# Delta rule's q, k and v turned by 32x32 blocks on DVE and over DRAM instead of by TensorE, with a new slab order

## The chip, the cores and the metric

The kernel runs on one core of a Trainium2 chip. The core has TensorE (PE in the profile, with its weight loads as PEld), VectorE (DVE), ScalarE (ACT), GpSimd (POOL) and SyncE (SP), which here only issues DMAs. Each works through its own instructions in program order. The metric is the device time of one execution in microseconds (us), given as the median of several runs.

## The reference

One layer of a hybrid encoder for 512 tokens and a model width of 1024, in float32. A single projection of the normalised input gives all branches; the two branches are merged, projected, and a gated embedding is added.

```python
h = rms_norm(x, norm_pre)
(aq, ak, av, az, dq, dk, dv, db, da, dz, gate_att, gate_dn) = split_cols(h @ w_in)
# branch A: GQA, 8 heads, 2 kv heads, rotary, softmax, * silu(az), @ w_br_att
# branch B, 8 heads of 128:
qkv = silu(short_conv(concat([dq, dk, dv]), conv_w))      # depthwise, 5 taps
qd = l2_norm(heads(cq)) * 128 ** -0.5
kd = l2_norm(heads(ck))
vd = heads(cv)
o_dn = chunk_gated_delta_rule(qd, kd, vd, g[0], beta[0]) + flip(chunk_gated_delta_rule(flipped ...))
y_dn = (rms_norm(o_dn, dn_norm) * silu(dz)) @ w_br_dn
mix = (sigmoid(gate_att) * y_att + sigmoid(gate_dn) * y_dn) @ w_out
x = x + rms_norm(mix, norm_post)
x = x + rms_norm(sigmoid(x @ w_ple_gate) * (p @ w_ple_proj), ple_norm)
```

The delta rule works in chunks. Within a chunk it inverts a unit triangular matrix built from k kᵀ, beta and the decay; between chunks it carries a state. It therefore needs k and v in two forms or in the one that the convolution doesn't give: the convolution and the products k kᵀ and k qᵀ want the channel on the partitions, the scans want the token there, and the l2 norm is a sum over channels.

## The kernel before, in words

**Precision.** A large product is made of three matmuls: each float32 operand is split into a high part (`hi`, rounded to fp32r) and a remainder (`lo`), and lo·hi, hi·lo and hi·hi are summed. `gemm_t` (L529 to L531) does so for a *slab*: 128 output columns for all 512 tokens, eight steps of three 128x512 matmuls, the result with channels on partitions and tokens along the row. Weights come by DMA into `wraw`, ACT rounds them into `whi`, and DVE or POOL subtracts to give `wlo` (L102 or L97).

**Order.** No loop of the hardware sets the order. While the program is written, a planner (`Flow`) keeps a clock and a calendar of each engine. Each part of the kernel is a generator that asks for a time (`at`), for an event of another part (`ev`) or for a buffer (`get`); the part with the smallest priority number that can go on goes on. An operation is entered at the first free place of its engine, with a duration written in the code, and the instructions come out in that order. `ORDER` lists the slabs of the main stream, which has the last priority and fills PE wherever nothing else is ready; `PR` holds priorities; `COOL` and `HOT` say how much later DVE may be than POOL before a weight split goes to POOL, outside and inside of the substitution.

**Branch B.** Heads 0 to 3 are group 0, heads 4 to 7 group 1. `conv_job` multiplies the slab of one head's q, k or v; `conv_tail` then works on the 128 channels x 512 tokens in PSUM:

1. `conv_silu2`: five taps (ACT one, DVE four), tanh on ACT, one product on DVE. The result stays with channels on partitions, in `kT` or `qT`, or in a tile `f2` for v.
2. `transposed` (L758 to L764): four PE transposes of 128x128 into one PSUM bank of the pool `mm`.
3. For q and k, ACT squares the transposed bank and DVE sums over channels (`ssk`, `ssq`); for k, ACT also copies the bank to `kn`. For v, DVE multiplies the bank by the norm `nk` of k into `nv`.

`k_stats` and `q_stats` make the norms of a group of four heads out of the sums, on POOL. `phase_a` then multiplies k kᵀ and k qᵀ (L942, L947), scales by the decay, inverts 32x32 blocks by a *substitution* of 30 steps of two DVE instructions (L975, L977), with a trip through DRAM ahead (`dB`) and behind (`dW`), and joins the blocks by small matmuls (L1019, L1032, L1052, L1067). `phase_b` is the scan of four chunk pairs in each direction (L1101 to L1162); it reads `kn` and `nv`, and puts its right side r and the product w into tiles of the pool `c2` (four buffers). Group 1 follows when group 0 is done. Slabs of the main stream stand between all of these on PE.

The step on which the rest depends most closely: the first matmul of the joined blocks, L1019, waits for DVE's transposes of the blocks that come back from DRAM.

Of the kernel before, what the change touches and what calls it, by code (L numbers as in the profile page):

```python
# [17 lines left out]
NT = 4  # L18
# [17 lines left out]
class Flow:  # L36
# [87 lines left out]
    def run(self):  # L124
        while self.parts:
# [38 lines left out]
ydn4 ydn3 ydn6 ydn0 ydn1 yatt5 yatt2 yatt6 yatt1 yatt7 yatt0 yatt4 yatt3 out0 out1 pg0  # L164
pg1
"""
OUT0 = 'ydn4 ydn3 ydn0 ydn0'
# [12 lines left out]

@with_exitstack
def layer(ctx, tc, x, xT, pw0, wp1, wt, wba, wn, rows, qkn, hd16, npost, pnorm, dnorm, cs, out):
# [39 lines left out]
    def const(shape, name, dt=F32):  # L222
        return sb.tile(shape, dt, tag=name, bufs=1, name=name)
# [50 lines left out]
                           pattern=[[pat, 128]], channel_multiplier=cm)  # L274
        return m

    two = const([64, 32], "two")
    pool.tensor_add(two, ident[0:64, 0:32], ident[0:64, 32:64])
    m_le = mask("m_le", -1, 1, 0)
    m_ge = mask("m_ge", 1, -1, 0)  # L280
    m_gt = mask("m_gt", 1, -1, -1)
# [451 lines left out]
        return max(t, te)  # L733


    ssk = const([128, 2, 4, 4], "ssk")
    ssq = const([128, 2, 4, 4], "ssq")
# [20 lines left out]
    def transposed(src):  # L758
        yield "get", "mm"
        o = bank("mm", [128, 4, 128])  # L760
        for c in range(NT):
            pe.transpose(o[:, c, :], src[:, c * 128:(c + 1) * 128], ident)
        yield "pe", 0.436
        return o  # L764

    def sumsq(pt, dst, dep=0.0):
# [4 lines left out]
        free("f2", t)  # L771
        return ta, t

    def conv_tail(kind, hd, po, nke):
        g, h = hd // 4, hd % 4
        yield "get", "f2"
        y = tile("f2", [128, 512])
        if kind == "dv":
            yield "get", "f2"
            dst = tile("f2", [128, 512])  # L780
            row = 16 + hd
        else:
# [4 lines left out]
        yield "at", t + 0.3  # L787
        pt = yield from transposed(dst)
        if kind == "dv":
            free("f2")  # L790
# [5 lines left out]
        ta, t = yield from sumsq(pt, (ssk if kind == "dk" else ssq)[:, g, :, h])  # L796
        if kind == "dk":
            ta = A(0.5, ta, act.copy, kn[g][:, :, h, :], pt)
        free("mm", ta)
        return t  # L800

    def k_stats(g, evs, dec):
        for e in evs:
            yield "ev", e
        yield "ev", dec
        t = G(0.2, 0.0, pool.tensor_scalar, out=nk[:, g], in0=ssk[:, g], scalar1=4.0 * EPS, scalar2=None, op0=ALU.add)
# [11 lines left out]
    def q_stats(g, evs):  # L818
        for e in evs:
            yield "ev", e  # L820
        return rsqrt(16, 0.0, rq[:, g], 1.0, 4.0 * EPS, float(128 ** -0.5), ssq[:, g])

    conv_ev, stat_ev = {}, {}
    conv_ready = {(k, g): Event() for k in ("dk", "dq", "dv") for g in range(2)}
# [41 lines left out]
    def prep(g, d):  # L866
# [11 lines left out]
        for c in range(NT):  # L878
# [23 lines left out]
                t = Q(2, t, E1[c], E)  # L902
            tE[g, d, c] = t
        if away:
            free("u16", t)
# [19 lines left out]
    def phase_a(g):  # L925
# [8 lines left out]
        for h in range(4):  # L934
            yield "ev", conv_ev["dq", 4 * g + h]
        k_, q_ = kT[g], qT[g]
        for c in range(NT):
            cc = slice(c * 128, (c + 1) * 128)
            yield "get", "aux"
            kk = bank("aux", [128, 4, 128])  # L940
            for h in range(4):
                pe.matmul(kk[:, h, :], k_[:, h, cc], k_[:, h, cc], start=True, stop=True)  # L942
            yield "pe", 0.9
            yield "get", "aux"
            qk = bank("aux", [128, 4, 128])
            for h in range(4):
                pe.matmul(qk[:, h, :], k_[:, h, cc], q_[:, h, cc], start=True, stop=True)  # L947
            yield "pe", 0.9
            for d in range(2):
                E = LT[d][:, 4 * c:4 * c + 4, :]  # L950
                t = V(0.62, tE[g, d, c], dve.tensor_mul, AT[g][d][:, 4 * c:4 * c + 4, :], qk, E)
                t = V(0.62, t, dve.tensor_mul, E, kk, E)
            free("aux", t)
            free("aux", t)

        dB, dW = dram(f"dB{g}", [128, 32, 32]), dram(f"dW{g}", [128, 32, 32])
        yield "get", "c2"
# [29 lines left out]
        free("blk", t)  # L987
        free("blk", t)
        free("blk", t)
        VT = []  # L990
        for i in range(2):
            yield "get", "blk"
            VT.append(tile("blk", [128, 16, 64]))
            G(0.95, 0.0, pool.memset, VT[i], 0.0)
        cx, tx = [], []
        for i in range(2):
            yield "get", "c2"
# [4 lines left out]
        for q in range(4):  # L1002
            r, lc = r32(q), r32(q % 2)
            t0 = A(0.53, tx[0], act.copy, LT[0][r, :, r], cx[0][r])
            t1 = V(0.6, tx[0], dve.transpose, VT[0][r, :, lc], cx[0][r])
        free("c2", max(t0, t1))
        for q in range(4):
            r, lc = r32(q), r32(q % 2)
            t0 = A(0.53, tx[1], act.copy, VT[1][r, :, lc], cx[1][r])
            t1 = V(0.6, tx[1], dve.transpose, LT[1][r, :, r], cx[1][r])  # L1010
        free("c2", max(t0, t1))
        yield "at", max(t0, t1) + 0.3

        combos = [(0, 0, 1), (0, 2, 3), (1, 1, 0), (1, 3, 2)]
        yield "get", "aux"
# [69 lines left out]
    def phase_b(g, d, ae, st8):  # L1085
        yield "ev", ae
        yield "ev", conv_ready["dv", g]
        for h in range(4):
            yield "ev", conv_ev["dv", 4 * g + h]
        yield "ev", stat_ev["q", g]  # L1090
        o = oo[g]
        tS = 0.0
# [320 lines left out]

    def q_done():
        for b in range(2):
            for t in range(NT):
# [8 lines left out]
    sm = const([128, 4, 4, 8], "sm")  # L1425
    ya = [None, None]

    def att_head(h):
# [485 lines left out]
```

## Time and profile before

| | |
|---|---|
| median of 3 runs | 762.31 us (762.13 to 762.71) |
| the profiled execution | 762.67 us, span 760.9 us |
| granted TensorE clock | 0.997 of full speed |
| DMA | 102.59 MB in 54472 packets, mean 135 GB/s |

The profile is of one execution. "Busy" is the time in which an engine worked on an instruction; matmuls overlap, so the distance between their starts tells more of PE than their durations. Rows of groups read: line, engine, operation, output<-input, shapes, count, then busy us and mean ns of one, then the idle time of that engine just before them and what ended it. The chain of waits is followed back from the last instruction. Line 122 and line 102 are those of helpers that record most operations, so such rows are told apart by their tiles.

### The profile page before, as it was taken

The page shows a single profiled execution, that of the slowest core. Times are in us where ns is not written, and L with a number is a line of the kernel's source. Part 1 is how long each engine was busy: PE and PEld are TensorE (multiplying, and loading weights), DVE is VectorE, ACT ScalarE, POOL GpSimd, SP SyncE. Part 2 cuts the span into 40 slices and gives each one's busy share as a digit, 9 for nine tenths or more (in the row PEclk, how much of TensorE's full clock was granted, in tenths as well). Part 3 has the DMA queues.
Part 4 walks back from the last instruction along what each step waited for, and adds up shares of the span by engine and source line. Part 5 has one row for each costly group of instructions (what it writes and reads, how often), then busy time and mean ns, then how long its engine had stood idle before and what let it go on. Part 6 is the DMA issues. An engine that isn't in the chain of part 4 may idle for free.

```text
span 760.9 us, 11834 instructions
## 1 busy us (share of the span) xinstructions
PE 746.0 (98%) x4505; PEld 624.7 (82%) x4505; DVE 465.1 (61%) x906; ACT 345.7 (45%) x644; POOL 307.8 (40%) x277
## 2 busy tenths in 40 slices
PE   8999999999999999999999999999999999999995
PEld 7788888878789888888798888888888888888885
DVE  4587788796955667894864535447666743313434
ACT  6668535543644264424442245335665623332422
POOL 4845762003322264202711246657454434661501
PEclk9999999999999999999999999999999999999998
DMA  9861338618111237554311134425335255552323
GB/s 346 300 196 60 113 92 280 205 61 235 39 61 42 70 111 189 178 167 118 113 56 42 56 103 134 158 91 194 111 97 166 72 193 205 187 169 104 97 72 108
DMA packets 54472, 102.59 MB, mean 135 GB/s; under 512 B 21072, under 2 KB 22032, under 8 KB 54416
## 3 DMA queue, kind: packets, MB, share of 16 engines
q1 hardware_dynamic: 54128, 101.58, 41.3%
q8 instruction: 35, 0.57, 0.3%
q10 hardware_dynamic: 288, 0.26, 0.1%
q14 instruction: 21, 0.17, 0.1%
HBM read 82.92 MB, written 18.91 MB: 134 GB/s over the span
## 4 chain that ended last, share of the span: by engine, by line
PE 88%; DMA 3%; DVE 3%; ACT 2%; issue 1%; POOL 1%; SPq 0%; POOLq 0%; DVEq 0%; ACTq 0%
PE mm L529 16%; PE mm L531 16%; PE mm L530 16%; PE mm L550 4%; PE mm L549 4%; PE mm L548 4%; PE mm L567 2%; PE mm L568 2%; PE mm L566 2%; PE aux L1121 2%; PE mm L1476 2%; PE aux L1153 2%; PE aux L1101 1%; PE aux L1112 1%; PE aux L1139 1%
## 5 line engine op out<-in xcount | busy, mean ns | idle before, releaser
L102 POOL TENSOR_TENSOR wlo<-wraw,whi 128x1024 fp32r<-128x1024 f32 x52 | 124.7, 2397 | 255.9 <-ACT whi L122 225.3
L529 PE MATMUL mm<-u,wlo 128*128 128x512 f32 x504 | 204.7, 406 | 2.2 <-DVE f L122 1.2
L531 PE MATMUL mm<-u,whi 128*128 128x512 f32 x504 | 197.2, 391 | 0.0
L530 PE MATMUL mm<-u,whi 128*128 128x512 f32 x504 | 196.5, 390 | 0.0
L529 PEld LDWEIGHTS mm<-u,wlo 128*128 128x128 f32 x504 | 94.8, 188 | 21.2 <-issue 2.0
L531 PEld LDWEIGHTS mm<-u,whi 128*128 128x128 f32 x504 | 94.6, 188 | 20.8
L530 PEld LDWEIGHTS mm<-u,whi 128*128 128x128 f32 x504 | 95.0, 188 | 17.0
L122 ACT CAST whi<-wraw 128x1024 fp32r<-128x1024 f32 x64 | 67.2, 1050 | 86.7 <-PE mm L531 55.8
L122 DVE SCALAR_TENSOR_TENSOR f<-mm,cw,f 128x510 f32<-128x510 f32 (+1 forms) x96 | 71.7, 747 | 20.7 <-ACT f L122 18.1
L102 POOL TENSOR_TENSOR u<-wraw,u 128x1024 fp32r<-128x1024 f32 x23 | 55.1, 2399 | 21.5 <-ACT u L122 21.4
L122 DVE TENSOR_TENSOR u<-aux,u 128x512 f32<-128x512 f32 (+2 forms) x60 | 39.3, 670 | 23.7 <-ACT u L122 15.4
L548 PE MATMUL mm<-u,u 128*128 128x512 f32 (+1 forms) x136 | 52.0, 382 | 0.0
L550 PE MATMUL mm<-u,u 128*128 128x512 f32 (+1 forms) x136 | 51.4, 378 | 0.0
L549 PE MATMUL mm<-u,u 128*128 128x512 f32 (+1 forms) x136 | 51.3, 377 | 0.0
L122 ACT COPY c<-aux 128x512 f32<-128x512 f32 x18 | 10.6, 590 | 55.0 <-DVE f L122 35.0
L122 ACT CAST u<-aux 128x512 fp32r<-128x512 f32 (+1 forms) x28 | 15.6, 556 | 39.9 <-PE aux L1649 13.0
L122 ACT ACTIVATE f<-mm 128x512 f32<-128x512 f32 (+1 forms) x38 | 21.1, 566 | 23.5 <-PE mm L550 8.7
L566 PE MATMUL mm<-whi,u 128*128 128x512 f32 x80 | 31.6, 395 | 0.0
L567 PE MATMUL mm<-wlo,u 128*128 128x512 f32 x80 | 31.3, 391 | 0.0
L568 PE MATMUL mm<-whi,u 128*128 128x512 f32 x80 | 31.2, 390 | 0.0
L122 ACT ACTIVATE mm<-f 128x512 f32<-128x512 f32 x24 | 14.5, 602 | 34.3 <-DVE f L122 33.0
L550 PEld LDWEIGHTS mm<-u,u 128*128 128x128 f32 x136 | 25.6, 188 | 4.8
(255 smaller groups left out, 1452.6 us busy)
## 6 DMA issues: line engine op xcount, KB each, us to landing
wraw<-in_wt_dram SPq DMA_DIRECT2D x60, 512.0 KB, 3.5
wraw<-in_wn_dram SPq DMA_DIRECT2D x28, 512.0 KB, 3.9
u<-in_wt_dram SPq DMA_DIRECT2D x12, 512.0 KB, 5.7
u<-CI SPq DMA_DIRECT2D x16, 256.0 KB, 6.3
u<-in_x_dram SPq DMA_DIRECT2D x4, 512.0 KB, 6.9
u<-in_xT_dram SPq DMA_DIRECT2D x4, 512.0 KB, 8.2
eD<-u SPq DMA_DIRECT2D x8, 256.0 KB, 8.0
gate_dz<-go SPq DMA_DIRECT2D x8, 256.0 KB, 2.1
```

The costliest lines, as they stand in the source:

```text
L102: ins = fn(*a, **k)
L122: fn(*a, **k)
L529: pe.matmul(o, lo[:, k, :], mh(k), start=(k == 0), stop=False)
L530: pe.matmul(o, hi[:, k, :], ml(k), start=False, stop=False)
L531: pe.matmul(o, hi[:, k, :], mh(k), start=False, stop=(k == 7))
L548: pe.matmul(o, b, hi, start=(i == 0), stop=False)
L549: pe.matmul(o, a, lo, start=False, stop=False)
L550: pe.matmul(o, a, hi, start=False, stop=(i == 7))
L566: pe.matmul(o[t], b, hi, start=(k == 0), stop=False)
L567: pe.matmul(o[t], a, lo, start=False, stop=False)
L568: pe.matmul(o[t], a, hi, start=False, stop=(k == 7))
L1121: pe.matmul(pw[:, h, :], Vm[g][d][:, 4 * c + h, :], r[:, h, :], start=True, stop=True)
```

## The change

- The 24 conv tails have no PE transposes any more. DVE transposes the 128x512 result in 32x32 blocks (`small_blocks`): in each 32-row strip of channels, every 32 tokens become rows.
- For k and v this tile `T` is written to DRAM with 2 KB per partition, and read back by four DMAs, one for each 32-row strip of the target, in pieces of 512 bytes, into a *landing* tile (`turned`). The landing tile is taken from the pool `c2`. From there ACT or POOL copies k to `kn` (`land_k`), and ACT (four instructions with a scale per partition) or POOL multiplies v by `nk` into `nv`, both in the layout that the scans read.
- The sums of squares are taken of the block-transposed tile: ACT squares, DVE sums 32 channels at a time into partial sums (`partk` for k, the tile `sm` for q). Once for each group and kind, four fp32 matmuls with the 128x32 selector `four` add up the four strips and give [token, head] sums in a PSUM bank (`sums`). DVE reads the bank into `nk` or `rq`.
- `phase_b` also waits for the copies of k (`kn_ev`).
- Some times that the planner hands on are now the latest of several (`ready`, `tm`, `tv`), where it was the last one entered.
- The slab order, `OUT0`, the priorities and `HOT` have new numbers.

```diff
 ORDER = """
-dq3 dk2 dq2 dk0 dk3 dq0 dk1 dq1 dz2 dk7 dq6 dz3 dv2 dv1 dv3 dz0
-dq4 gB7 dz7 dv0 dz5 az5 gA6 gA0 dz1 dq5 dk5 dk4 gA1 dk6 gA7 gA3
-dq7 gB0 az7 gB6 gB1 dv4 az6 dv6 gB2 gA2 az2 gB4 kv dv7 dv5 gB5
-az0 gA4 vec dz4 az3 gB3 q0 dz6 gA5 q1 az4 az1 free_h ydn2 ydn5 ydn7
...
+dk0 vec dk1 dq0 dq1 dq3 dq2 dk2 az4 dk3 dv1 dv3 dq5 dv0 dq7 dz7
+dk5 dv2 az3 dz5 dz3 az6 gB2 gB4 dz0 az0 gA3 dk4 dk7 dz4 dq6 dq4
+gA4 dk6 gA6 gB5 dz1 dz2 dv7 dv4 dv5 gA0 az1 gA5 gB0 gA2 dv6 az2
+gA1 kv gA7 gB7 az7 gB6 gB3 q0 gB1 dz6 q1 az5 free_h ydn0 ydn6 ydn7
...
-PR = dict(dec=6, dm1=5, y=2, conv=9, gate=1, kv=2, q=4, head=9, ple=6, prep=6, tab=2)
+PR = dict(dec=8, dm1=8, y=7, conv=9, gate=0, kv=9, q=4, head=6, ple=1, prep=2, tab=1)
+WIDE = 2.0
+LAND = "c2"
-COOL, HOT = 2.5, 0
+COOL, HOT = 2.5, -1.5
...
+    def small_blocks(src, dep):
+        T = tile("f2", [128, 4, 4, 32])
+        return T, V(0.64, dep, dve.transpose, T.rearrange("p a j q -> p j a q"), src)
+
+    def turned(T, dep, name, dst):
+        B = dram(name, [4, 32, 4, 128])
+        tw = Q(2, dep, B.rearrange("P i a n -> (P i) a n"), T.rearrange("p a j q -> p a (j q)"))
+        t = tw
+        for a in range(4):
+            t = Q(WIDE, tw, dst[32 * a:32 * a + 32].rearrange("p P j q -> p P (j q)"), B[:, :, a, :].rearrange("P i n -> i P n"))
+        return tw, t
...
-        pt = yield from transposed(dst)
+        yield "get", "f2"
+        T, t = small_blocks(dst, t)
         if kind == "dv":
-            t = V(0.62, 0.0, dve.tensor_mul, nv[g][:, :, h, :], pt,
-                  nk[:, g, :, h].unsqueeze(2).to_broadcast([128, 4, 128]))
-            free("mm", t)
+            yield "get", LAND
+            L = tile(LAND, [128, 4, 4, 32])
+            tw, t = turned(T, t, f"B{kind}{hd}", L)
...
+            t = either(t, ("POOL", 1.1, pool.tensor_mul, o_, i_, nk[:, g, :, h]...),
+                       ("ACT", 1.25, scaled))
...
+        ta = A(0.5, t, act.activation, sq, T, AF.Square)
+        t = V(0.62, ta, dve.reduce_sum, parts_[kind][:, g, :, h, :], sq, axis=AX.X)
...
+    def sums(kind, g):
+        yield "at", F.now + 0.3
+        yield "get", "mm"
+        o = bank("mm", [128, 16])
+        for a in range(4):
+            pe.matmul(o[32 * a:32 * a + 32, :], four, parts_[kind][:, g, a].rearrange("p h j -> p (h j)"), start=True, stop=True)
+        yield "pe", 0.44
+        return o.rearrange("p (h j) -> p j h", h=4)
```

Three places of the new order bear on the prediction.

**PE, a conv tail's transposes and what replaces them.** Before, PE has the four transposes of v's tile `f_189` in the midst of a slab (`mm_1582` is the slab's bank; "waits" names the engine waited for):

```order
L531 MATMUL mm_1582<-u_14_130,whi_1527 128x512
L762 MATMUL mm_1603<-ident,f_189_1530 128x128 [waits DVE_49,PE_49]
L762 MATMUL mm_1603<-ident,f_189_1530 128x128 x3
L529 MATMUL mm_1582<-u_15_131,wlo_1528 128x512
L530 MATMUL mm_1582<-u_17_133,whi_1527 128x512
```

Now a slab runs on, and once per group and kind there are the selector's matmuls:

```order
L536 MATMUL mm_998<-u_14_131,whi_943 128x512
L862 MATMUL mm_1018<-partk,four 32x16 [waits DVE_49,PE_49]
L862 MATMUL mm_1018<-partk,four 32x16 x3
L534 MATMUL mm_998<-u_14_131,wlo_944 128x512
L535 MATMUL mm_998<-u_16_133,whi_943 128x512
```

All 24 blocks of L762 are gone, and four groups like the second have come.

**DVE, between the steps of group 0's substitution.** Before, early steps (L975, L977) with a conv tail (`f_159`), v's product with `nk`, a decay add (L893), a gate (`go`) and a weight split among them:

```order
L977 TENSOR_TENSOR blk_1153<-blk_1153,blk_1154 128x29x2 [waits DVE_49]
L122 SCALAR_TENSOR_TENSOR f_160_1243<-mm_1195,f_159_1242 128x512 [waits Activation_49]
L122 TENSOR_TENSOR u_136_1088<-mm_1256,nk 128x4x128 [waits PE_49]
L893 TENSOR_TENSOR u_155_1224<-u_155_1224,cj 128x512 [waits Pool_49]
L122 SCALAR_TENSOR_TENSOR go_1306<-go_1306,mm_1244 128x512 [waits DMAHW0_49]
L97 TENSOR_TENSOR wlo_1305<-u_29_210,whi_1304 128x1024 [waits DMAHW4_49,PE_49,Activation_49]
L975 TENSOR_TENSOR blk_1154<-blk_1152,blk_1153 128x28x3 [waits DVE_49]
```

Now, with the steps at L1049 and L1051:

```order
L97 TENSOR_TENSOR wlo_1460<-wraw_1314,whi_1459 128x1024 [waits DMAHW5_49,Activation_49]
L122 SCALAR_TENSOR_TENSOR go_1461<-go_1461,mm_1407 128x512 [waits Activation_49]
L1049 TENSOR_TENSOR blk_1329<-blk_1327,blk_1328 128x28x3 [waits DVE_49]
L1051 TENSOR_TENSOR blk_1328<-blk_1328,blk_1329 128x28x3 [waits DVE_49]
L1049 TENSOR_TENSOR blk_1329<-blk_1327,blk_1328 128x27x4 [waits DVE_49]
L1051 TENSOR_TENSOR blk_1328<-blk_1328,blk_1329 128x27x4 [waits DVE_49]
```

In the 30 steps there are now 8 splits, 5 gates and 6 decay adds and no conv tail; before there were 10 splits, 12 taps and 4 last products of conv tails, 4 gates, 4 decay adds, 3 products with `nk` and a sum. On PE, between the last k qᵀ product of group 0 and the first product of the joined blocks, there were 375 matmuls of 512 columns and 24 transposes, and there are now 318 matmuls of 512 columns.

**DVE and POOL, the scan's first r and the landing buffers.** On DVE the scan of group 0 begins (L1181 writes r into `c_274`), with waits for four DMA queues and POOL:

```order
L122 TENSOR_TENSOR f_265_2288<-aux_2281,dj 128x512 [waits Activation_49]
L122 TENSOR_TENSOR f_268_2297<-aux_2290,dj 128x512 [waits DMAHW1_49,Activation_49]
L1181 SCALAR_TENSOR_TENSOR c_274_2327<-aux_2322,nec,u_99_845 128x128 [waits DMAHW5_49,DMAHW6_49,DMAHW0_49,DMAHW7_49,PE_49,Pool_49]
L1181 SCALAR_TENSOR_TENSOR c_274_2327<-aux_2322,nec,u_99_845 128x128 x3
L122 SCALAR_TENSOR_TENSOR f_278_2339<-mm_2158,cw,f_278_2339 128x510 [waits Activation_49]
```

On POOL, the copies that set the landing buffers `c_238` and `c_250` (k of two heads of group 1) free stand behind weight splits:

```order
L102 TENSOR_TENSOR wlo_1963<-wraw_1852,whi_1962 128x1024 [waits DMAHW5_49,Activation_49,Pool_49]
L102 TENSOR_TENSOR wlo_2156<-u_29_211,whi_2155 128x1024 [waits DMAHW6_49,Activation_49]
L102 COPY u_158_1248<-c_238_1922 128x4x128 [waits DMAHW6_49,DMAHW7_49,DMAHW5_49,DMAHW0_49]
L102 COPY u_158_1248<-c_250_2122 128x4x128 [waits DMAHW4_49,DMAHW5_49,DMAHW3_49,DMAHW2_49]
L102 TENSOR_TENSOR wlo_2338<-wraw_2038,whi_2337 128x1024 [waits PE_49,DMAHW1_49,Activation_49,Pool_49]
```

Before, the scans shared `c2` with no landing.

More of the change, by code (lines that the diff above doesn't have):

```diff
@@ L275, in mask @@
         return m
-    two = const([64, 32], "two")
-    pool.tensor_add(two, ident[0:64, 0:32], ident[0:64, 32:64])
+    four = const([128, 32], "four")
+    pool.tensor_add(four, ident[:, 0:32], ident[:, 32:64])
+    for i in (2, 3):
+        pool.tensor_add(four, four, ident[:, 32 * i:32 * i + 32])
+    two = four[0:64, :]
     m_le = mask("m_le", -1, 1, 0)
@@ L795, in conv_tail @@
             return t
-        ta, t = yield from sumsq(pt, (ssk if kind == "dk" else ssq)[:, g, :, h])
         if kind == "dk":
-            ta = A(0.5, ta, act.copy, kn[g][:, :, h, :], pt)
-        free("mm", ta)
-        return t
+            yield "get", LAND
+            L = tile(LAND, [128, 4, 4, 32])
+            tw, t2 = turned(T, t, f"B{kind}{hd}", L)
+            spawn(land_k(hd, L, t2), PR["conv"])
+            yield "at", t - 0.2
+            yield "get", "f2"
+            sq = tile("f2", [128, 4, 4, 32])
+        else:
+            sq = T
@@ new lines, in conv_tail, with land_k @@
+        ta = A(0.5, t, act.activation, sq, T, AF.Square)
+        if kind == "dk":
+            free("f2", max(ta, tw))
+        t = V(0.62, ta, dve.reduce_sum, parts_[kind][:, g, :, h, :], sq, axis=AX.X)
+        free("f2", t)
+        return t
+    kn_ev = [Event() for _ in range(8)]
+    def land_k(hd, L, t):
+        yield "at", t - 0.5
+        o = kn[hd // 4][:, :, hd % 4, :].rearrange("p j (P q) -> p j P q", P=4)
+        t = either(t, ("ACT", 0.57, act.copy, o, L.rearrange("p P j q -> p j P q")), ("POOL", 0.7, pool.tensor_copy, o, L.rearrange("p P j q -> p j P q")))
+        free(LAND, t)
+        kn_ev[hd].set(t)
@@ L804, in k_stats @@
             yield "ev", e
+        o = yield from sums("dk", g)
+        t = V(0.2, 0.0, dve.tensor_scalar, out=nk[:, g], in0=o, scalar1=4.0 * EPS, scalar2=None, op0=ALU.add)
+        free("mm", t)
         yield "ev", dec
-        t = G(0.2, 0.0, pool.tensor_scalar, out=nk[:, g], in0=ssk[:, g], scalar1=4.0 * EPS, scalar2=None, op0=ALU.add)
         t = V(0.25, t, dve.reciprocal, kinv[:, g], nk[:, g])
@@ L820, in q_stats @@
             yield "ev", e
-        return rsqrt(16, 0.0, rq[:, g], 1.0, 4.0 * EPS, float(128 ** -0.5), ssq[:, g])
+        o = yield from sums("dq", g)
+        t = V(0.2, 0.0, dve.tensor_copy, rq[:, g], o)
+        free("mm", t)
+        return rsqrt(16, t, rq[:, g], 1.0, 4.0 * EPS, float(128 ** -0.5))
     conv_ev, stat_ev = {}, {}
@@ L904, in prep @@
         if away:
+            t = max(tE[g, d, c] for c in range(NT))
             free("u16", t)
@@ L936, in phase_a @@
         k_, q_ = kT[g], qT[g]
+        ready = 0.0
         for c in range(NT):
@@ L948, in phase_a @@
             yield "pe", 0.9
+            tm = 0.0
             for d in range(2):
```

46 lines of the change are left out of this document (30 added, 16 removed).

## The prediction

> **What bounds the kernel now.** I read the page first (busy time, slices, chain), then PE's waits, then the timelines of the places that the change touches.
>
> The page's head, busy time by engine, PE's and DVE's slices, and the chain's shares by engine:
>
> ```profile
> span 760.9 us, 11834 instructions
> PE 746.0 (98%) x4505; PEld 624.7 (82%) x4505; DVE 465.1 (61%) x906; ACT 345.7 (45%) x644; POOL 307.8 (40%) x277
> ...
> PE   8999999999999999999999999999999999999995
> ...
> DVE  4587788796955667894864535447666743313434
> ...
> PE 88%; DMA 3%; DVE 3%; ACT 2%; issue 1%; POOL 1%; SPq 0%; POOLq 0%; DVEq 0%; ACTq 0%
> ```
>
> PE is busy in every slice but the first and the last, and the chain that ended last runs through it for 88%. A busy PE may still stand behind a pipelined matmul, so I ask how fast it issues, and what it waited for (us in total, times, longest):
>
> ```profile
> PE mm L762 <- DVE f L122: 1.5, 1, 1.5
> PE mm L1777 <- POOL ident masks.py:199: 1.4, 1, 1.4
> PE mm L529 <- DVE f L122: 1.2, 1, 1.2
> PE mm L529 <- DVE wlo L97: 0.5, 2, 0.3
> ```
>
> These are the largest of nine rows. So PE has almost no idle time: the kernel is bound by the number of PE instructions, and what leaves PE shortens it one for one, unless PE waits somewhere new. What shortens DVE, ACT or POOL is worth nothing by itself.
>
> **What the change removes from PE.** Each of the 24 conv tails (q, k, v of 8 heads) now has four 128x128 transposes by matmul at L762. Around one block (start, duration):
>
> ```profile
> 55.82 0.39 PE L530 MATMUL mm<-u,whi 128*128 128x512 f32 x1
> ...
> 56.96 0.60 PE L762 MATMUL mm<-ident,u 128*128 128x128 f32 x4
> 57.31 0.48 PE L529 MATMUL mm<-u,wlo 128*128 128x512 f32 x1
> 57.62 0.39 PE L530 MATMUL mm<-u,whi 128*128 128x512 f32 x1
> ```
>
> The first two rows are five 512-column matmuls apart, 1.14 us, so one takes 0.228. From L762's start to the second matmul behind it are 0.66 us; less one matmul, the block costs 0.43. The chain of waits books it the same way (start, us, what), and L762's own rows give the count, 64 + 32:
>
> ```profile
> 57.12 0.44 PE mm L762 x4
> ...
> L762 PE MATMUL mm<-ident,u x64: 270/272/327, 38.1 to 266.5; 128*128 128x128 f32 x64
> L762 PE MATMUL mm<-ident,f x32: 270/272/328, 117.2 to 389.2; 128*128 128x128 f32 x32
> ```
>
> 24 x 0.44 = **-10.6 us**. With them goes L762's one wait for DVE, **-1.5 us** (bounds 0, if DVE's lateness shows at the next dependent instruction, and -1.5).
>
> **What it adds to PE.** Four groups of four fp32 matmuls with the 32-column selector `four` (L862, a new line), which fold the partial sums of squares. No row has this shape. Chain rows of small fp32 matmuls, in which one written matmul is two instructions:
>
> ```profile
> 40.79 0.81 PE aux L701 x8
> ...
> 200.76 0.81 PE aux L1032 x54
> ```
>
> At L701's pace (128 weight columns, 32 moving) a group of 8 instructions is 0.81 us; at L1032's (32x32) it is 8 x 0.015 = 0.12. Four groups: 0.5 to 3.2. K is 128 as in L701, so I take 0.81: **+3.2 us**.
> The Trainium skill, page "TensorE: Matmul & The Clock Gate", section "LDWEIGHTS (loading the stationary operand)", says that loading weights takes time by their columns, P / 1.2 ns, whatever K is: 107 ns for 128 columns, which the trace's 0.10 per instruction of L701 bears out, but 27 ns for 32. By that rule the term would be an estimated 0.9 us, and the sum below 2.3 us lower.
>
> **What it adds elsewhere.** Nearest rows on DVE: the block transpose (of 32 partitions), the multiply by nk that goes, the sum that stays, and a conv tap:
>
> ```profile
> L122 DVE STREAM_TRANSPOSE blk<-c 32x512 f32<-32x512 f32 x8 | 5.6, 702 | 8.4 <-DMA c<-dW 8.3
> L122 DVE TENSOR_TENSOR u<-mm,nk 128x512 f32<-128x512 f32 x8 | 5.5, 682 | 0.3 <-PE mm L762 0.3
> L122 DVE TENSOR_REDUCE ssk<-f 128x4 f32<-128x512 f32 x8 | 5.4, 680 | 0.2 <-ACT f L122 0.2
> L122 DVE SCALAR_TENSOR_TENSOR f<-mm,cw,f 128x510 f32<-128x510 f32 x48 | 35.7, 745 | 19.1 <-ACT f L122 18.1
> ```
>
> DVE: 24 x 0.70 - 8 x 0.68 = +11.4 us; the lanes work side by side in every other row, so 128 partitions should cost what 32 do (bounds: 0.70, and four times that if not). v's scaling moves to ACT, four pieces per head as at L918; k's copies, one per head as now, go to ACT or POOL, where the nearest row is a 128x512 TENSOR_SCALAR:
>
> ```profile
> L918 ACT ACTIVATE u<-u,Nj 128x128 f32<-128x128 f32 x44 | 13.2, 388 | 0.0
> ...
> L102 POOL TENSOR_SCALAR u<-u,sm 128x512 f32<-128x512 f32 x16 | 11.1, 697 | 22.5 <-DVE sm L122 16.3 <-PE aux L1468 6.0
> ```
>
> 32 x 0.39 = +12.4 us on ACT, four copies of 0.7 on POOL. All of this, POOL's two more adds for `four` and four 128x16 reads of the folded sums on DVE lie under PE's 98% and cost nothing while DVE (61%) and ACT (45%) keep ahead. If DVE's cover were gone, up to its 11.4 us would reach PE. The tables of numbers act through the order alone and are costed there, below.
>
> The landing: k and v go to DRAM (256 KB) and back in four reads of 64 KB, 80 more issues on SP. Nearest rows (KB each, us to landing):
>
> ```profile
> gate_dz<-go SPq DMA_DIRECT2D x8, 256.0 KB, 2.1
> gi<-gate_dz SPq DMA_DIRECT2D x8, 256.0 KB, 4.2
> dW<-blk SPq DMA_DIRECT2D x2, 512.0 KB, 3.4
> c<-dW SPq DMA_DIRECT2D x4, 256.0 KB, 5.1
> ```
>
> 2.1 + 4.2 to 5.1 = 6.3 to 7.2 us. Each first read waits on SP for its write, and behind it stand the next weight fetch or gate store. PE's nine waits name no DMA and weights come slabs ahead, so 2 us on SP cost 0 (bounds 0 and 2.1 per head, if that lead is gone). Only the scans read the landed k and v, tens of us after the last v of their group: 0; the price if a scan waits is in the last rival.
>
> **Where a stall can come back: the substitution of group 0.** The slab order moves conv tails away from it. In the present kernel PE's last q-k products of group 0 (L947) and the first product of the inverted blocks (L1019) stand here, DVE's last transposes before L1019 next, then DVE's busy time in three legs (start of the products to the first step, the 30 steps, the way back through DRAM), then the steps' two instructions in the middle leg, and one row of that leg:
>
> ```profile
> 105.41 1.05 PE L947 MATMUL aux<-u,u 128*128 128x128 f32 x8
> ...
> 196.54 1.29 PE L1019 MATMUL aux<-blk,u 32*32 32x32 f32 x128
> ...
> 193.70 2.89 DVE L122 STREAM_TRANSPOSE u<-c 32x512 f32<-32x512 f32 x4
> ...
> 106.40:122.00 15.60, 13.39 (x19) 1.00 0.74 212
> 122.00:180.00 58.00, 49.53 (x100) 1.00 0.53 178
> 180.00:196.60 16.60, 9.99 (x15) 1.00 0.47 115
> ...
> 122.00:180.00 58.00, 9.86 (x30) 1.00 0.53 178
> ...
> 122.00:180.00 58.00, 9.88 (x30) 1.00 0.53 178
> ...
> L893 DVE TENSOR_TENSOR u<-u,cj 128x512 f32<-128x512 f32 x4 | 2.8, 690 | 3.8 <-POOL u L102 3.6
> ```
>
> L1019 starts as DVE ends (196.6): no slack now. The order holds 375 matmuls of 512 columns and six transpose blocks between the two: 375 x 0.228 + 6 x 0.44 = 88 us of PE work as cover for a chain of 90 us. In the changed order it is 318 matmuls, 72.5 us. The chain shrinks too: the steps' leg has 49.5 - 9.9 - 9.9 = 29.8 us of other DVE work now; the new order leaves 8 weight splits, 5 gates and 6 decay adds there:
>
> ```profile
> L97 DVE TENSOR_TENSOR wlo<-wraw,whi 128x1024 fp32r<-128x1024 f32 x12 | 14.9, 1239 | 3.4 <-ACT whi L122 3.4
> L122 DVE SCALAR_TENSOR_TENSOR go<-go,mm 128x512 f32<-128x512 f32 x24 | 16.3, 681 | 5.7 <-ACT go L122 5.5 <-DMA go<-gate_gB 0.2
> ```
>
> 8 x 1.24 + 5 x 0.68 + 6 x 0.69 = 17.5 us. The first leg gains two block transposes and two sums less one multiply, 1.4 + 1.4 - 0.7 = +2.1, of which part fits its 2.2 us of idle: take +1.5. So the chain needs 15.6 + 1.5 + 19.7 + 17.5 + 16.6 = 70.9 us plus idle time between the steps. That is 8.5 us now (58.0 - 49.5); L893's wait for POOL is 3.8 of it and stays, the rest may go. With 3.8, 74.7 against 72.5: PE waits **+2.2 us** (bounds 0 and, with all 8.5, 6.9). For group 1 the order gives the opposite: 327 matmuls and 16 transposes instead of 288 and 24, 8 us more cover, and 6 us more DVE work. No term.
>
> **Sum.** -10.6 - 1.5 + 3.2 + 2.2 = -6.7 us. The profiled execution took 762.67, the median is 762.31, 0.36 lower: 762.31 - 6.7 = **755.6 us**. Start and tail keep their instructions: 0.
>
> **Rivals.**
> (1) *More goes than I count* (17%): the selector matmuls at L1032's pace (0.5) and no wait at the substitution: -10.6 - 1.5 + 0.5 = -11.6, **750.7**. For it: the weights are 32 columns wide. Against it: every fp32 row with K = 128 stands at 0.10 per instruction.
> (2) *The wait takes the place of the transposes* (12%): the substitution keeps all its idle time (6.9) and DVE's lateness of 1.5 shows there instead: -10.6 + 3.2 + 6.9 = -0.5, **761.8**, no change that can be told. For it: no slack at L1019 now, and 15.6 us less PE work in front. Against it: 12.3 us less DVE work between the steps.
> (3) *The landing buffers hold up the scan* (11%), slower. The landing tiles are taken from the four `c2` buffers in which the scans put r and w. In the new order DVE's first r of group 0 takes the buffer of the landing of one k of group 1, which POOL copies out behind a weight split:
>
> ```profile
> L102 POOL TENSOR_TENSOR wlo<-wraw,whi 128x1024 fp32r<-128x1024 f32 x52 | 124.7, 2397 | 255.9 <-ACT whi L122 225.3
> ```
>
> If that r comes before the landing has begun, PE waits for write, read, split and copy, 2.1 + 5.1 + 2.4 + 0.7 = 10.3 us: -6.7 + 10.3 = +3.6, **765.9**. It decides above 6.7 us. Against it: by the order's matmuls some 20 us of PE work lie between that k's transpose and that r, twice the price.
> The Trainium skill speaks against the change here: "VectorE: DVE Perf Modes", section "The three transpose paths", keeps 128x128 transposes for TensorE and calls a strided plain DMA 19 times slower than the crossbar's. No run here shows that factor: c<-dW, rearranged in 128-byte pieces, lands in 5.1 us against 4.2 for gi<-gate_dz in long ones.
>
> **How the numbers follow.** The forecast case has 60%, 752.5 to 759.5, for the price of the selector and the idle time. With (1) at 750.7 and most of (2), the range is **749.5 to 761.9**; it leaves out (3) and the edges. This kernel's measurement tells some 0.2%, 1.5 us, from no change: faster means below 760.8. The forecast and (1) are faster, and of (2) a part: 80%. Same, most of (2): 9%. Slower, (3): 11%.
>
> **What would show it.** L762's counterpart has no conv rows; L862 stands 32 times, in four groups of 0.8 us. PE's instructions fall by 64. PE's waits show one row of about 2 us at the first product behind the substitution (L1094 or its neighbour), none for a landing. The block transpose at 128 partitions takes 0.70 us, and the landing 6 to 7. The forecast is wrong if PE's idle time grows by more than 6 us, at the substitution or in the scans.

## The result, and the profile after

| | before | after |
|---|---|---|
| median | 762.22 us (761.99 to 762.71) | 755.03 us (754.48 to 755.96) |
| ratio to before, 95% interval | | 0.9906 (0.9889 to 0.9923) |
| profiled span | 760.9 us | 754.2 us |

The change makes the kernel 7.2 us faster; 755.6 was predicted. The head of the page of the changed kernel, its slices of PE and of the granted TensorE clock (PEclk, in tenths) and the shares of its chain, to be set against the lines of before:

```profile
span 754.2 us, 11916 instructions
PE 738.5 (98%) x4441; PEld 618.3 (82%) x4441; DVE 475.3 (63%) x924; ACT 353.2 (47%) x668; POOL 315.6 (42%) x284
...
PE   9999999999799999999999999999999999999996
...
PEclk9999999999899999999999999999999999999999
...
PE 85%; DVE 4%; DMA 4%; ACT 3%; issue 1%; POOL 1%; SPq 0%; POOLq 0%; DVEq 0%; ACTq 0%
```

PE has the 64 instructions less that the change promises (96 transposes go, 32 selectors come) and is still busy for 98%. One slice has fallen to 7, the eleventh (188 to 207 us), where the substitution of group 0 comes back. The granted clock has a dip in the same slice; before, only the last slice had one. PE's waits in the changed kernel, all rows (us in total, times, longest):

```profile
PE mm L534 <- POOL wlo L102: 2.8, 2, 2.3
PE aux L1094 <- ACT blk L122: 1.8, 2, 1.0
PE mm L1853 <- POOL ident masks.py:199: 1.4, 1, 1.4
PE aux L1107 <- issue: 1.0, 1, 1.0
PE mm L534 <- DVE wlo L97: 0.5, 2, 0.3
PE mm L656 <- POOL u L102: 0.4, 1, 0.4
PE aux L1215 <- ACT c L122: 0.3, 1, 0.3
```

They add up to 8.2 us; the nine rows of before had 6.7. L762's wait is gone, and so is the 1.2 us at L529 behind DVE. In their place two new ones stand side by side at the substitution: L1094, the first product of the inverted blocks, behind ACT's copies, and a slab's first matmul (L534) behind POOL's part of its weight split. The new work by its own rows, one group of selector matmuls within a slab and then the block transposes of q and k on DVE:

```profile
82.39 0.39 PE L536 MATMUL mm<-u,u 128*128 128x512 f32 x1
82.71 0.26 PE L862 MATMUL mm<-sm,four 128*32 128x16 f32 x8
82.89 0.50 PE L534 MATMUL mm<-u,wlo 128*128 128x512 f32 x1
83.23 0.39 PE L535 MATMUL mm<-u,whi 128*128 128x512 f32 x1
```

```profile
L122 DVE STREAM_TRANSPOSE f<-u 128x512 f32<-128x512 f32 x16 | 11.2, 702 | 0.0
```

From the matmul in front of the group to the second one behind it are 0.84 us, where two undisturbed steps take 0.46, so the group costs 0.38 us; the other three, read in the same way, cost as much. The block transpose takes 0.70 us on 128 partitions, as predicted from 32. The landing takes about what was estimated: the writes 2.3 to 2.8 us, each read 2.2 to 2.5 us (medians from issue to landing), and the fourth read is issued 1.3 us behind the first, which makes 6.1 to 6.3 us against 6.3 to 7.2.

### The profile page after: what moved, and what is told of

It reads as the page before. It is cut to its first block, busy times and chain, and to the rows that moved or that the text cites. A ratio compares the mean times of both kernels' runs of the same rounds, so it can differ in the third digit from the quotient of the medians.

```text
span 754.2 us, 11916 instructions
## 1 busy us (share of the span) xinstructions
PE 738.5 (98%) x4441; PEld 618.3 (82%) x4441; DVE 475.3 (63%) x924; ACT 353.2 (47%) x668; POOL 315.6 (42%) x284
## 4 chain that ended last, share of the span: by engine, by line
PE 85%; DVE 4%; DMA 4%; ACT 3%; issue 1%; POOL 1%; SPq 0%; POOLq 0%; DVEq 0%; ACTq 0%
PE mm L534 14%; PE mm L535 14%; PE mm L536 14%; PE mm L555 4%; PE mm L553 4%; PE mm L554 4%; PE mm L571 3%; PE mm L572 3%; PE mm L573 3%; PE aux L1197 2%; PE aux L1229 2%; DMA u<-CI 2%; PE mm L1552 2%; DVE f L122 2%; PE aux L1215 2%; PE aux L1188 1%
## 5 line engine op out<-in xcount | busy, mean ns | idle before, releaser
L534 PE MATMUL mm<-u,wlo 128*128 128x512 f32 x504 | 204.3, 405 | 3.3 <-POOL wlo L102 2.8
L534 PEld LDWEIGHTS mm<-u,wlo 128*128 128x128 f32 x504 | 95.2, 189 | 23.2 <-POOL wlo L102 3.3
L122 ACT COPY c<-aux 128x512 f32<-128x512 f32 x18 | 10.6, 587 | 47.7 <-DVE f L122 28.7
L102 POOL TENSOR_SCALAR_AFFINE_SELECT u<-u 128x512 f32<-128x512 f32 x16 | 10.1, 640 | 49.8 <-DMA u<-CI 37.5
```

Source lines behind the costliest of these rows:

```text
L102: ins = fn(*a, **k)
L122: fn(*a, **k)
L534: pe.matmul(o, lo[:, k, :], mh(k), start=(k == 0), stop=False)
```

## The experiments

Unless another reference is named, a time is set against the changed kernel's 755.03 us, and a ratio against the kernel before, which ran beside each call (761.7 to 762.5 us). "Order held" means that the planner was told nothing of the edit, so that every instruction of the changed kernel keeps its place.

### What the transposes and the selectors are worth on PE

**e1** puts four transposes per conv tail back as a step of the planner, with a result that nobody reads.

```diff
         T, t = small_blocks(dst, t)
+        yield "at", t
+        yield "get", "mm"
+        o_ = bank("mm", [128, 4, 128])
+        for c in range(NT):
+            pe.transpose(o_[:, c, :], dst[:, c * 128:(c + 1) * 128], ident)
+        yield "pe", 0.436
+        free("mm")
```

> The changed kernel with the 24 blocks of four PE transposes put back behind the block transposes; nobody reads their result, all else is the change's. Theory (PE is the bound, each PE instruction that leaves is worth its time): 24 x 0.44 = +10.6 us over the changed kernel's 755.0, and up to 1.5 more if PE again waits there for DVE: 765 to 767, some 3 to 4 us slower than the kernel before. Rival (the gain came from the new order, and PE has room for the transposes): within 3 us of 755.

Measured: 779.42 us (777.7 to 782.05), ratio 1.0232 (1.0202 to 1.0261). That is 24.4 us more, over twice the price of the 96 instructions. The step takes a bank and a moment of the planner's clock, so the whole order comes out differently, and PE finds new waits, the largest `L534 <- POOL wlo` with 4.9 us in three places. Nothing about the transposes follows from it; the question goes to e5.

**e5** has the same 96 instructions with the order held.

```diff
         o = bank("mm")
+        for c in range(4 if name[0] in ("dk", "dq", "dv") else 0):
+            pe.transpose(o[:, c * 128:(c + 1) * 128], ident, ident)
         for k in range(8):
```

> The changed kernel with four 128x128 fp32 transposes by matmul (of the identity, into the bank of the product that follows, unread) ahead of each of the 24 conv products: the 96 instructions of the old L762 are back on PE and every other instruction of every engine keeps its place. One-for-one theory (24 x 0.44 = 10.6): 765.0 to 766.0 us. Rival, that most of e1's loss of 24 us came with the instructions themselves: 775 or more. Second rival, that transposes hide behind neighbouring matmuls and the gain of the change came from its order: 755 to 758.

Measured: 763.76 us (762.37 to 767.25), ratio 1.0024 (1.0009 to 1.0039). The head of its page:

```profile
span 764.2 us, 12112 instructions
...
PE 748.8 (98%) x4537; PEld 627.4 (82%) x4537; DVE 475.2 (62%) x924; ACT 352.9 (46%) x668; POOL 315.7 (41%) x284
```

The 96 transposes cost 8.7 us of the median, 10.0 us of the span and 10.3 us of PE's busy time, and with them the changed kernel is no faster than the one before. The one-for-one theory stands, with a median a little below its 765 to 766. The two profiled executions differ in more than the transposes: e5's named waits add up to 8.0 us against 8.2, and its slower stretch of matmuls behind the substitution's wait (see below) costs 1.3 us against 2.1. With both set right, the 96 transposes cost some 11 us, so the term of 10.6 was not too high. Between e1 and e5 lie 15.7 us: most of it is the price of the other order, but e1's transposes also read the conv tail's result and can wait for it, while e5's read a constant.

**e2** runs each selector matmul five times.

```diff
-        for a in range(4):
+        for a in [0, 1, 2, 3] * 5:
             pe.matmul(o[32 * a:32 * a + 32, :], four, ...
```

> The changed kernel with the selector's matmuls of each group done five times over (128 more PE instructions, the same result). By the prediction's price, 0.10 us per instruction, +12.8 us: 768. By the profile after, in which the 32 instructions stand about 0.02 us apart, and by the rule that a weight load costs by its columns (27 ns for 32), +3 to +3.5 us: 758 to 758.5.

Measured: 755.60 us (755.05 to 756.16), ratio 0.9920 (0.9905 to 0.9934). 128 PE instructions more cost 0.6 us, 0.005 us each, which is less than the runs of one kernel differ among themselves and below both theories. The weight loads of half of them, and one group as PE ran it:

```profile
L862 PEld LDWEIGHTS mm<-sm,four x80: 106/113/113, 82.0 to 240.6; 128*32 128x32 f32 x80
...
81.99 0.54 PE L862 MATMUL mm<-sm,four 128*32 128x16 f32 x40
82.46 0.50 PE L534 MATMUL mm<-u,wlo 128*128 128x512 f32 x1
```

A group of 40 holds PE for 0.47 us from its start to the next matmul's, a group of 8 (above) for 0.18: by this a further instruction costs 0.009 us. So most of the 0.38 us that a group of 8 costs is the break in the slab's stream, not the count of its instructions. Each weight load is still recorded with 106 to 113 ns, so they must overlap. Four in a row go to four different groups of 32 columns; that this is why they overlap was not varied.

### Code and order apart

**e3** is the kernel before with the new tables; **e9** adds the corrected times that came with the change, on which that order rests (`ready`, `tm`, `tv`, the maximum over the spilled chunks, the event of q's statistics); **e4** is the changed code with the old tables. In e3 two of DVE's transposes of group 1 run at 372.48 us, before POOL clears the tile that they write (from 373.95); in e9 all four wait for that. So e3 loses two blocks of the inverse, its time is that of a changed computation, and e9 is the one to go by.

```diff
 # e3, e9: tables of the change in the kernel before     # e4: tables of before in the change
-COOL, HOT = 2.5, 0
+COOL, HOT = 2.5, -1.5
 # e9 also, among others
-        yield "at", max(t0, t1) + 0.3
+        yield "at", max(t0, t1, ready) + 0.3
```

> The kernel before (PE transposes, no landing) with the change's slab order, priorities and HOT. Theory (the transposes on PE are the gain): PE's work is that of before, so 762 plus or minus 4, whatever the order. Rival (the order is the gain): 755 to 757.

> The kernel before (transposes by matmul, no landing) with the changed kernel's tables and with the corrected times that came with the change (of the spilled E, of the products that free aux, of the blk memsets, of q's statistics), which e3 lacked. Theory that the tables were made for the changed code and give nothing by themselves: 762 to 775. Rival, that the order gives a good part of the 7 us by itself: 756 to 760.

> The change's code with the slab order, priorities and HOT of the kernel before. Theory: PE's work is the change's (-9.9 us), the waits are those of another order: 752 to 760. Rival (the order is the gain): 762 or more.

Measured: e3 768.59 us (766.19 to 770.7), ratio 1.0089 (1.0064 to 1.0114); e9 769.60 us (768.12 to 772.0), ratio 1.0108 (1.0083 to 1.0133); e4 775.18 us (773.02 to 777.83), ratio 1.0178 (1.0151 to 1.0205). Each half alone is slower than the kernel before, and e3 and e4 are above what their theories allowed. In e4 PE's instructions are those of the changed kernel, and most of the loss is in new waits (19.8 us named, against 8.2), the largest this row:

```profile
PE mm L534 <- POOL wlo L102: 7.3, 4, 3.5
```

So an order belongs to the durations and buffers of one program. The effect of the code without an order made for it cannot be read from e4, nor that of the order from e9.

### What hides DVE's new work

**e6** does each block transpose twice, order held.

```diff
-        return T, V(0.64, dep, dve.transpose, T.rearrange("p a j q -> p j a q"), src)
+        dve_t = lambda: [dve.transpose(T.rearrange("p a j q -> p j a q"), src) for _ in range(2)][-1]
+        return T, V(0.64, dep, dve_t)
```

> The changed kernel with each of the 24 block transposes on DVE done twice in a row, 16.9 us of DVE work more, order held. Theory that DVE has cover everywhere but at the substitution of group 0, whose chain takes in only two blocks: 755 to 757. Rival, that DVE's work reaches PE: 760 to 772.

Measured: 760.55 us (758.44 to 761.7), ratio 0.9978 (0.9967 to 0.9989): 5.5 us more, and the span of the profiled execution, the shortest of ten, 2.5 us more. Two of its PE waits:

```profile
PE mm L534 <- POOL wlo L102: 4.2, 3, 2.3
...
PE mm L534 <- DVE wlo L97: 1.1, 2, 0.8
```

The median is at the lower edge of the rival's range. Of some 17 us more DVE work a third or less reaches PE, by small waits, for weight splits above all and for the partial sums (L863, 0.6 us). DVE's cover is wide but not whole. That of the change's own 11.4 us some part also reaches PE is likely by this, but was not measured apart.

### What hides the landing

**e7** issues every transfer of the landing twice, one right behind the other.

```diff
+        class twice:
+            def dma_start(o, i):
+                sync.dma_start(o, i)
+                return sync.dma_start(o, i)
```

> The changed kernel with every transfer of the landing (16 writes of 256 KB, 64 reads of 64 KB) issued twice in a row on SP: the landed k and v come some 4 to 5 us later, 80 issues and 8 MB more, order held on the other engines. Theory that the landing has slack of tens of us: 754.5 to 756. Rival, that weight fetches behind it or the scans are held up: 2 us per head and more, 760 to 771.

Measured: 880.38 us (878.3 to 882.33), ratio 1.1548 (1.1518 to 1.1578). What SP waited for, the rows at the second transfers:

```profile
SPq L793 <- DMA c<-Bdv: 61.3, 32, 4.2
SPq L793 <- DMA c<-Bdk: 54.6, 32, 3.6
...
SPq L793 <- DMA Bdv<-f: 21.9, 8, 6.1
SPq L793 <- DMA Bdk<-f: 20.9, 8, 5.1
```

Both transfers write the same place, so the second waits on SP until the first has landed: 80 waits, 158.7 us in which SP issues nothing. The run does not measure the landing; it shows that SP's queue has no lead to pay for such waits, since the kernel is 125 us longer. Weight fetches stand behind, and PE's row `L534 <- POOL wlo` grows to 46.9 us. All of PE's named waits grow by 95.6 us and its busy time, with the same instructions, by 26.6; the mean granted clock is 0.940.

**e10** gives the second transfers places of their own, so that none waits.

```diff
+            def fn():
+                r = sync.dma_start(o, i)
+                sync.dma_start(o2, i)
+                return r
```

> The changed kernel with every transfer of the landing issued a second time into DRAM tensors of its own (16 writes, 64 reads, 80 issues on SP and 8 MB more), so that no second transfer waits for the first as in e7; order held on every other engine. Theory that e7's 125 us came from SP standing still between two transfers to one place, and that issues and bytes of the landing are hidden: 754.5 to 757. Rival, that issues on SP or bytes themselves hold up the weight fetches: 765 and more, up to e7's 880.

Measured: 779.31 us (778.95 to 781.39), ratio 1.0235 (1.0219 to 1.0251): 24.3 us more, so the rival holds. The largest wait is the first, at 65 us. SP and POOL ahead of it, in the changed kernel (timelines: start, us, what):

```profile
55.90 1.74 SPq L122 DMA_DIRECT2D c<-Bdk  x4
57.69 1.86 SPq L122 DMA_DIRECT2D u<-CI  x4
...
62.55 0.64 POOL L102 TENSOR_SCALAR_AFFINE_SELECT u<-u 128x512 f32<-128x512 f32 x1 [3.25 <-DMA u<-CI]
63.13 0.61 POOL L102 COPY u<-c 128x512 f32<-128x512 f32 x1
63.71 2.39 POOL L102 TENSOR_TENSOR wlo<-u,whi 128x1024 fp32r<-128x1024 f32 x1
```

and in e10:

```profile
64.28 0.53 SPq L794 DMA_DIRECT2D Bdk1y<-Bdk  x1
64.85 1.53 SPq L122 DMA_DIRECT2D u<-CI  x3
...
69.50 0.63 POOL L102 TENSOR_SCALAR_AFFINE_SELECT u<-u 128x512 f32<-128x512 f32 x1 [6.65 <-DMA u<-CI]
...
70.66 2.80 POOL L102 TENSOR_TENSOR wlo<-u,whi 128x1024 fp32r<-128x1024 f32 x1
```

The chain reads from the top. The landing's reads on SP, 0.44 us each in the changed kernel and 0.5 to 0.6 in e10, hold up the reads of the decay tables (`u<-CI`). POOL stands before its mask on such a table, with a weight split behind it, and PE's next slab waits for that split. In e10 all this is 7 us later, and PE's wait there is 8.0 us long.

The waits are not the whole loss. The profiled span of e10 is 23.0 us longer; PE's named waits make 15.9 of it (24.1 against 8.2), and the other 7.1 are PE's busy time, which grew with the instructions and their order unchanged. From 68 to 79 us, late in that wait and behind it, the granted clock is 0.50, and so it is for some us at three more waits; its mean is 0.981, against 0.994 in the changed kernel.

**e11** cuts each landing to one transfer from tile to tile, beside **e12**, the changed kernel once more.

```diff
-        tw = Q(2, dep, B.rearrange("P i a n -> (P i) a n"), T.rearrange("p a j q -> p a (j q)"))
+        tw = Q(2, dep, dst.rearrange("p P j q -> p P (j q)"), T.rearrange("p a j q -> p a (j q)"))
...
-            t = Q(WIDE, tw, dst[32 * a:32 * a + 32].rearrange("p P j q -> p P (j q)"), B[:, :, a, :].rearrange("P i n -> i P n"))
+            t = op("DMA", WIDE * 0.31, op("DGE", 0.46, tw, None) + 0.5, None) + 1.3
```

> The changed kernel with each of the 16 landings cut to one transfer from the transposed tile straight into the landing tile (no DRAM, no four reads: 64 issues on SP and the wait of SP for each write go; the blocks then stand in the wrong order, so the exchange of blocks is left out of what is computed), order held on the other engines. Theory that the landing is hidden in the changed kernel: 753.5 to 755.5. Rival, that the landing's issues on SP, which stand ahead of the decay tables' reads, already cost PE a few us in the changed kernel (e10 showed them 8 us late when doubled): 750 to 753.

> The changed kernel once more, unaltered, beside e11 on the same chip, so that e11 has its own reference: 754.5 to 756 by its earlier runs.

Measured: e11 752.53 us (750.95 to 752.97), e12 754.50 us (754.24 to 755.27). So the way over DRAM costs about 2.0 us against a single transfer, and the rival holds. PE's waits in e12, and then in e11:

```profile
PE mm L534 <- POOL wlo L102: 3.2, 2, 2.3
...
PE aux L1094 <- ACT blk L122: 1.4, 2, 1.0
```

```profile
PE mm L534 <- POOL wlo L102: 2.3, 1, 2.3
...
PE aux L1094 <- ACT blk L122: 0.8, 1, 0.8
```

The second wait for a split, the one at 65 us, is gone in e11. PE is 0.8 us earlier at 101 us for it, and the last operand of L1094 comes 1.9 us earlier (194.50 against 196.37).

### The wait at the substitution

The place in the changed kernel (timelines of ACT, POOL and PE, the last three rows with the first matmuls behind the wait):

```profile
191.78 2.51 ACT L122 COPY u<-c 32x512 f32<-32x512 f32 x4 [2.39 <-DMA c<-dW]
194.31 2.51 ACT L122 COPY blk<-c 32x512 f32<-32x512 f32 x4
196.84 1.04 ACT L122 CAST whi<-wraw 128x1024 fp32r<-128x1024 f32 x1
...
197.96 4.69 POOL L102 TENSOR_TENSOR wlo<-wraw,whi 128x1024 fp32r<-128x1024 f32 x2 [8.71 <-ACT whi L122]
...
194.65 0.25 PE L1094 MATMUL aux<-blk,u 32*32 32x32 f32 x4
195.69 0.22 PE L1094 MATMUL aux<-blk,u 32*32 32x32 f32 x2 [0.80 <-ACT blk L122]
196.87 1.24 PE L1094 MATMUL aux<-blk,u 32*32 32x32 f32 x122 [0.95 <-ACT blk L122]
200.37 0.79 PE L534 MATMUL mm<-u,wlo 128*128 128x512 f32 x1 [2.26 <-POOL wlo L102]
200.96 0.63 PE L535 MATMUL mm<-u,whi 128*128 128x512 f32 x1
201.38 0.63 PE L536 MATMUL mm<-u,whi 128*128 128x512 f32 x1
```

L1094 goes on as ACT's second four copies end (194.31 + 2.51 = 196.82). Behind those copies stands the cast of the next weights, behind the cast POOL's subtraction, and that is the row of 2.3 us at L534. The matmuls behind it are slow: they start 0.42 us apart, where 0.23 is usual, and the granted clock is 0.50 from 200 to 204 us.

**e8** gives the second four copies to POOL, order held.

```diff
-            t0 = A(0.53, max(tx[1], tv[1]), act.copy, VT[1][r, :, lc], cx[1][r])
+            t0 = A(0.53, max(tx[1], tv[1]), pool.tensor_copy, VT[1][r, :, lc], cx[1][r])
```

> The changed kernel with the second four of the eight block copies after the substitution (into the second blk tile, one group of four per half) moved from ACT to POOL, everything else in place. The profile of the changed kernel shows PE waiting 2.45 us for POOL's part of the next weight split, which waits for ACT's cast, which waits for the eight copies (2.5 us per four). Theory that this queue holds PE: the cast starts 2.5 us earlier, PE's wait for wlo falls from 2.45 to about 0.5, total 752.5 to 753.5. Rival, that PE there waits for DVE's transposes of the same tiles, which end later than the copies: within 0.5 us of the changed kernel, 754.5 to 755.5. Second rival: POOL's copies are slower than ACT's and delay both: 756 to 758.

Measured: 752.47 us (752.08 to 753.41), ratio 0.9872 (0.9857 to 0.9888). The same place on ACT, POOL and PE in e8:

```profile
193.56 1.05 ACT L122 CAST whi<-wraw 128x1024 fp32r<-128x1024 f32 x1
...
192.25 2.57 POOL L122 COPY blk<-c 32x512 f32<-32x512 f32 x4 [3.34 <-DMA c<-dW]
194.90 4.70 POOL L102 TENSOR_TENSOR wlo<-wraw,whi 128x1024 fp32r<-128x1024 f32 x2
...
197.31 0.50 PE L534 MATMUL mm<-u,wlo 128*128 128x512 f32 x1 [1.20 <-POOL wlo L102]
197.65 0.40 PE L535 MATMUL mm<-u,whi 128*128 128x512 f32 x1
...
207.84 2.08 PE L1127 MATMUL aux<-blk,u 64*64 64x64 f32 x62 [1.06 <-DVE blk L122]
```

PE's waits there fall from 1.8 to 0.3 us (L1094, now behind POOL's copies) and from 2.3 (the row has 2.26, not 2.45) to 1.2 us (L534 behind the split); a new one of 1.1 us comes at L1127, where PE now arrives before DVE. The forecast time holds, 2.6 us less, and e8 is faster than both kernels. But the waits alone don't give it: all named ones fall by 1.6 us (8.2 to 6.6) and the profiled span by 4.0. The rest is mostly the clock. In e8 it is 1.00 throughout this place, and from L534's start behind the wait to the second L534 behind the next small products (L1107) are 3.60 us; in the changed kernel there are 5.65, so the slow stretch costs 2.1 us. In e12, the changed kernel again, the stretch is shorter (5.05, 1.5 us). What e8 and a shorter landing give together was not tried.

## Why the prediction was right

The total came out within 0.6 us, though by errors that cancel.

- **What bounds the kernel: right.** PE's instructions set the time. e5 shows it at the same order: 96 instructions, 8.7 us of the median and 10.0 of the span.
- **Transposes, -10.6: right.** By e5, with its waits and slow stretch set apart, some 11 us.
- **L762's wait, -1.5: gone,** and it did not come back at DVE's next dependent instruction. No run took it alone. The 1.2 us at L529 behind DVE, which the sum left in place, went too.
- **Selectors, +3.2: mis-sized.** The four groups cost 0.38 us each, 1.5 in all. The step that failed is the price per instruction, taken from L701's row because K is 128: L701 has 128 weight columns, the selector 32 for each of four strips. L1032's row, which also puts out 32 columns at a time, gives the bound of 0.5, which is too low, since a group also breaks the slab's stream. The Trainium skill has a rule that the prediction missed: its page "TensorEngine Tiling (Array Packing)", section "Key Properties", says that tiles of the array work on their own and can load weights and multiply in parallel. e2 agrees. The price by columns that the prediction did weigh shows in no row: the recorded loads have 106 to 113 ns, and a further load with its matmul costs 5 to 9 ns.
- **DVE, +11.4 hidden: mostly.** By e6 the cover is not whole, so a cost of nothing was too low by an amount that stays open.
- **Landing, 0: wrong by 2.0 us** (e11). The transfer times were right together, and no scan waits for a landing. The step that failed is "behind it stand the next weight fetch or gate store": in front of group 0 it is the reads of the decay tables that stand behind, and they had no lead of slabs. PE's row names POOL and not a DMA, since the late transfer is three instructions up the chain. e10 shows how thin that cover is.
- **Substitution, +2.2: the place right, the reason wrong in part.** PE waits 1.8 us at L1094 and 2.3 at the slab behind. The length of the chain was right: from the end of group 0's last k qᵀ products (L1018, 121.02 + 1.05 us) to the last go of L1094 (196.87) are 74.8 us, against 74.7. Its last link was not: "L1019 starts as DVE ends: no slack now" was a coincidence. The second four of DVE's transposes write the diagonal blocks, which the first product does not read; its last operand comes from ACT's copies, which in the kernel before ended 2.0 us ahead of L1019 (196.54), as its timeline shows:

```profile
192.04 2.52 ACT L122 COPY blk<-c 32x512 f32<-32x512 f32 x4
```

  The second wait, the weight split queued behind these copies on ACT, was not in the prediction at all, and it is the larger one. Neither was the slow stretch of matmuls behind it, another 2.1 us: the place costs 6.2 us, not 2.2.
- **The balance** of the two profiled executions. Transposes -11.0 (e5), selectors +1.5, PE's named waits +1.5 (6.7 to 8.2), the slow stretch +2.1, and idle time of PE that no row names -0.7 (8.2 to 7.5). That makes -6.6, against the -6.7 by which the span shrank. So the forecast of -6.7 was met by luck in its size: the selectors were put 1.7 too high, the substitution 4.0 too low, and L529's 1.2 us were not in the sum.
- **The rivals.** (1) had the selectors at 0.5, too low, and no wait at the substitution, which is wrong. (2) wanted 6.9 us at the substitution, and with the slow stretch 6.2 came; it failed since L762's wait did not come back and the selectors cost less. (3) did not come: no row of PE names a scan's tile behind a landing.

## What to carry to other kernels

When an engine is full, the value of taking work off it is the work itself, but here only in an order made for the new program: the same code in the old order was 20 us slower than in its own, so test a price with the order held. Before calling a wait hidden, follow the operand that the first instruction really reads, and ask of each queue passed (SP and ACT here) what stands next in it and who waits for that; the stall shows under the name of the last link, not the first. Look at the matmuls behind a stall too: here their slower pace cost half as much again as the waits at the substitution (2.1 us beside 4.1). Copies that a critical product needs should not share an in-order engine with the next weights' cast, when another engine stands idle.

## What the hardware showed that was not expected

- Of the 32-column fp32 selector matmuls, with K of 128 and 16 moving columns, a further instruction cost 0.005 us by e2's time and 0.009 by its trace, a tenth or less of the 0.10 us of L701's rows, while a group of eight cost 0.38 by breaking a stream of large matmuls. A block of the old transposes cost hardly more, 0.43.
- Late in some waits of PE and behind them the granted clock was 0.50 for several us and large matmuls started 0.42 us apart instead of 0.23: from 199 to 205 us in the changed kernel, and four times in e10. Not every wait had this behind it: the row `L529 <- DVE f`, 2.1 us, is in e3 and in e9, and only e3 has a slow stretch there (316 to 320 us). What decides was not varied.
- DMA issues on SP are not free when they come in a row: 1.74 us for four in the changed kernel. Doubling them and their 8 MB cost 24.3 us (e10), where transfers that wait for each other cost 125 (e7). In e10's profiled execution, 7.1 us of the loss are PE's slower pace, not its waits. How the 24.3 divide between issues and bytes stays open.
- POOL's copies of 32x512 took 2.57 us for four, against ACT's 2.51.
